# A hybrid decoder layer with 32 experts on one core: first weights by the block, second expert matrices in 16 KB packets, λ later, last sums earlier

## The chip, the cores and the metric

One core of a Trainium2 chip. The metric is the device time of one execution in microseconds; the time before is the median of three runs. All inputs and weights are fp32 in HBM.

## The reference, cut to what matters

```python
mod = silu(c) @ ada_w + ada_b                       # c: 1024, ada_w: 1024 x 6144
sh1, sc1, gt1, sh2, sc2, gt2 = split(mod, 6)
h = rms_norm(x, pre_mix_norm) * (1 + sc1) + sh1     # x: 256 x 1024
proj = h @ w_in                                     # attention and RWKV columns
...
lam = exp(sum(lam_q1 * lam_k1)) - exp(sum(lam_q2 * lam_k2)) + lambda_init
...
y = concatenate([y_da, y_rw]) @ w_out
x = x + gt1 * rms_norm(y, post_mix_norm)

h = rms_norm(x, pre_ffn_norm) * (1 + sc2) + sh2
logits = h @ router_w + router_b
top_vals, top_idx = top_k(logits, 4)                # of 32 experts
gates = sum(one_hot(top_idx, 32) * softmax(top_vals)[..., None], axis=1)
def expert(acc, w1_e, b1_e, w2_e, b2_e, g_e):       # w1: 1024 x 2048, w2: 1024 x 1024
    hid = h @ w1_e + b1_e
    glu, lin = min(hid[:, ::2], 7), clip(hid[:, 1::2], -7, 7)
    return acc + g_e[:, None] * ((glu * sigmoid(1.702 * glu) * (lin + 1)) @ w2_e + b2_e)
x = x + gt2 * rms_norm(sum over the experts, post_ffn_norm)
```

## The kernel before

**Mixer.** The program first computes the modulation rows sh1 and sc1, a pair of feature blocks of 128 at a time. `load_first(kp)` (L164) loads for pair `kp` two pieces of `ada_w` (shift and scale, 1 MB each, in runs of 1 KB) and two rows of blocks of `w_in` (896 KB each). `mod_rows` multiplies `cs` (silu of c) with a piece, `mod_copy` brings the row to SBUF, `mod_cols_first` turns it into columns `g1` and `sh1`, and `mod_x(k)` modulates block `k` of the transposed x into two halves, a high and a low one (`hpart`). `split_first` (L398) splits a block of `w_in` in the same way on ScalarE, VectorE and GpSimd. `proj_first(k, fs)` is the product of block `k`: 54 matmuls into seven PSUM banks, which were opened by a matmul with zeros. `warm(n)` issues `n` matmuls of ones whose result is not used. The order of PE, DVE and ACT in this part is that of the code. Attention and the RWKV heads follow; λ is worked out by five VectorE operations and one Exp (L729 to L736) when the last projection columns are shifted (`shift`).

**Experts.** The 32 experts run one after the other, the tokens of each gathered into 64, 32 or 96 slots (`kind`). An expert's weights are 12 MB: w1 as four pairs of blocks of 2 MB, w2 as four pieces of 1 MB. They go through a ring of 18 slots of 1 MB (`ring`, `slot`), and SyncE issues all loads in order (`load_expert`, L1577; pairs at L1598, w2 pieces at L1602). Each waits until PE has read what its slots held. The first four experts load w1 in single blocks.

Per expert: `gemm1` (eight blocks `k`, bias ahead of it), `act_of` (the clamped SwiGLU), `act_tr` (transposes), `gemm2` (eight blocks), `scatter` (products with `back` that spread the rows over the tokens, added into `acc` by VectorE at L1789). `gemm1` and `gemm2` call functions of a table `between` after certain blocks. In the last expert (p = 31) `sum_so_far(i)` opens the two final banks of token tile `i` with `acc` and the b2 term; the last `scatter` closes them, and `last_norm` writes the output. What its `gemm2` has between its blocks (`not nxt`):

```python
        elif not nxt:
            warm(24)
            between = {0: lambda: scatter(*done[:2], which=(0,)), 1: lambda: scatter(*done[:2], which=(1,)),
                       5: lambda: sum_so_far(0), 3: lambda: sum_so_far(1)}
```

All matmuls have the line of the helper `mm` (L104), transposes that of `tr` (L107). Tiles are named by use: `pair` are weight buffers, `xs` the gathered tokens, `aTt` the transposed activations, `ys` an expert's result.

Of the kernel before, what the change touches and what calls it, by code (L numbers as in the profile page):

```python
# [20 lines left out]
D = 1024  # L21
# [27 lines left out]
OVER_AT = 8  # L49
WARM = (34, 4, 0, 6, 8)  # L50
LEAD = 5
# [24 lines left out]
def hybrid_layer_kernel(ctx, tc, x, c, positions, ada_w, ada_b, pre_mix_norm, post_mix_norm,  # L76
# [26 lines left out]
    def mm(o, l, r, start=True, stop=True):  # L103
        PE.matmul(o, l, r, start=start, stop=stop)  # L104
# [60 lines left out]
    def load_first(kp):  # L165
# [23 lines left out]

    first = load_first(0)  # L190
    jp = pro.tile([128, 128], I32)
# [185 lines left out]
    def mod_cols_first(kp):  # L377
# [31 lines left out]

    ada, w = first  # L410
    warm(WARM[0])
    xj = pair((1024,), (1024,))
    norm_x(xj)
    x_tr(0, xj[0])
    mod_rows(0, 0, ada)
    x_tr(1, xj[1])
    mod_rows(0, 1, ada)
    col_tr(0)
    V.tensor_scalar(pc[:, cols["sc1"][0]:cols["sc1"][0] + 8], pc[:, cols["sc1"][0]:cols["sc1"][0] + 8], 1.0, None,
                    op0=OP.add)  # L420
    mod_copy(0)
    parts = []
    sf = split_first(w[:1], (G, V), (0, 512, 1024, 1536, 1792))
    for _ in range(2):
        next(sf)
    mod_cols_first(0)
    rwb = {}
    ORDER = (0, 2, 4, 6, 8, 10, 12)
    for f in ORDER:
        rwb[f] = (bankb if f in (12, 8, 10) else bank)()  # L430
        mm(rwb[f], zero, zero[:, 0:1].to_broadcast([128, 512]), True, False)
    warm(WARM[1], bankc)
    next(sf)
    mod_x(0)
    for _ in sf:
        pass
    mod_x(1)
    for _ in split_first(w[1:], (V, V)):
        pass
    first_order.close()  # L440


    mu1 = pro.tile([128, 14], F32)

    def shift(dst, p, f):
        S.activation(dst, p, AF.Copy, scale=mu1[:, f:f + 1])  # L446
        V.scalar_tensor_tensor(dst[:, 1:], p[:, 0:T - 1], col("mu", f), dst[:, 1:], op0=OP.mult, op1=OP.add)  # L447

    def proj_first(k, fs):
        xh, xl = hpart(k)  # L450
        for f in fs:
            for q in (f, f + 1):
                wh, wl = (t[:, q * 128:(q + 1) * 128] for t in parts[k])
                for n, (l, r) in enumerate(((wh, xh), (wh, xl), (wl, xh))):
                    mm(rwb[f][:, (q - f) * T:(q - f + 1) * T], l, r, False, k == KC - 1 and n == 2 and q > f)

    proj_order = tc.manual_schedule(engines={mybir.EngineType.PE, mybir.EngineType.DVE, mybir.EngineType.Activation})
    with proj_order:
        for kp in range(3):
            ada, w = load_first(kp + 1)  # L460
            k = 2 * kp
            proj_first(k, ORDER)
# [265 lines left out]
    lam2 = pro.tile([128, 2], F32)  # L728
    V.tensor_tensor(lamt[:, 0], lamt[:, 0], lamt[:, 1], op=OP.mult)  # L729
    V.tensor_tensor(lamt[:, 2], lamt[:, 2], lamt[:, 3], op=OP.mult)  # L730
    V.tensor_reduce(lam2, lamt[:, 0:4:2], axis=AX.X, op=OP.add)
    with tc.issue_after(first_act.ins):
        S.activation(lam2, lam2, AF.Exp)
    nlam = pro.tile([128, 1], F32)
    V.tensor_tensor(nlam, lam2[:, 1:2], lam2[:, 0:1], op=OP.subtract)
    V.tensor_scalar(nlam, nlam, LAMBDA_INIT, None, op0=OP.subtract)  # L736
    sub_c = pro.tile([128, 1], F32)
# [838 lines left out]

    def load_expert(e, s1_, s2_, single=False):  # L1577

# [5 lines left out]
        for j in range(4):  # L1584
# [148 lines left out]

    W2_ORDER = (0, 2, 1, 3)

    def gemm2(aTt, w2s, gates_of, kind, between=None):

        ks = [2 * s + j for s in W2_ORDER for j in range(2)]
        b64 = bank() if kind != 32 else None
# [35 lines left out]

    def scatter(ys, back, which=range(NT)):
        for i in which:
            for n in range(2):
                h = slice(64 * n, 64 * n + 64)
                if i in ends:  # L1780
                    for m, (j, y) in enumerate(ys):
                        mm(ends[i][n], back[h, j, i], y[h], False, m == len(ys) - 1)
                    continue
# [139 lines left out]
    for p in range(EXPERTS):  # L1923
        kind = kind_at(p)
        w1s, w2s = weights
        if p + 1 < EXPERTS:
            weights = [], {}
            rest_of_load = load_expert(expert_of(p + 1), *weights, p + 1 < SINGLE)
# [12 lines left out]
        if p + 1 < EXPERTS:  # L1941
# [14 lines left out]
            if 96 not in (kind, kind1):  # L1956
                bs = gemm1_bias(onehot(p + 1), kind1)
            between[5] = lambda: back1.append(prep_back(nxt[1], gate1, kind1, picked(p + 1)))
        back1 = []
        if p == 0:  # L1960
# [5 lines left out]

            between[3], between[5] = between[5], rest_of_first
# [18 lines left out]
        if p == OVER_AT:  # L1986
            last = nc.values_load(n_ov, min_val=0, max_val=MAX_OVER)
    scatter(*done[:2])
    pe_order.close()
# [66 lines left out]
```

## Time and profile before

| | us |
|---|---|
| median of 3 runs (lowest, highest) | 1189.94 (1188.75, 1190.77) |
| profiled execution, its own time | 1190.35 |
| its span in the trace | 1188.5 |
| PE busy | 1078.3 (91%) |
| VectorE busy | 412.1 (35%) |
| ScalarE busy | 227.6 (19%) |
| chain that ended last: DMA, PE | 45%, 45% |
| mean granted TensorE clock | 0.972 |

The span runs from the first to the last instruction; the run's own time has 1.85 us more around it. Busy shares are means over stages. The chain is followed back from the last instruction to what released each step. In rows, an arrow `<-` reads "out from in", and `x16` is a count of instructions.

### The profile page before, as it was taken

How to read it: one execution, taken by the hardware profiler on the slowest of the kernel's cores; microseconds unless marked ns; L12 is line 12 of the kernel's file. 1: busy time of each engine (PE TensorE's matmuls, PEld its weight loads, DVE VectorE, ACT ScalarE, POOL GpSimd, SP SyncE). 2: the span in 40 equal slices, each digit the busy share in tenths (PEclk: the TensorE clock that was granted, in tenths of full speed). 3: DMA queues.
4: the chain of work that ended last, by engine and by line, in shares of the span. 5: the costliest groups of instructions: out<-in, count | busy, mean ns of one | idle time of the engine just before them, and what ended most of it. 6: DMA issues, size and time to landing. Idle time of an engine off the chain costs nothing.

```text
span 1188.5 us, 17092 instructions
## 1 busy us (share of the span) xinstructions
PE 1078.3 (91%) x6717; PEld 507.3 (43%) x6717; DVE 412.1 (35%) x1114; ACT 227.6 (19%) x529; POOL 53.7 (5%) x100
## 2 busy tenths in 40 slices
PE   8999999999997877999988999988999999798765
PEld 6976667654343232233443233433333434333211
DVE  5688469852331212122323112312212223121203
ACT  4374353312011001010111010111010101101001
POOL 1331020000000000000000000000000000000000
PEclk8999999999999988999999999999999999999978
DMA  9862778899999999999999999999999999999991
GB/s 336 317 235 71 280 270 330 326 371 383 423 424 426 426 425 426 425 426 424 425 425 426 424 426 427 422 426 426 423 426 426 425 426 425 425 426 425 423 382 48
DMA packets 60101, 453.15 MB, mean 381 GB/s; under 512 B 7850, under 2 KB 16105, under 8 KB 23154
## 3 DMA queue, kind: packets, MB, share of 16 engines
q1 hardware_dynamic: 57970, 449.88, 91.9%
q0 software_dynamic: 1856, 2.13, 0.6%
q8 instruction: 54, 0.88, 0.3%
q14 instruction: 29, 0.24, 0.1%
q10 hardware_dynamic: 192, 0.02, 0.0%
HBM read 450.94 MB, written 1.06 MB: 380 GB/s over the span
## 4 chain that ended last, share of the span: by engine, by line
DMA 45%; PE 45%; DVE 6%; ACT 2%; issue 1%; SPq 0%; DVEq 0%; ACTq 0%
DMA pair<-in_moe_w 44%; PE bank L104 32%; PE bankb L104 10%; PE bankc L104 3%; DMA pair<-in_ada_w 1%; DVE pair L316 1%; PE bank L107 1%; ACT aTt L1731 0%; PE bankb L107 0%; DVE pair L447 0%; ACT xs L1656 0%; DVE w L316 0%; DVE pair L1195 0%; ACT pair L446 0%; DVE w L766 0%
## 5 line engine op out<-in xcount | busy, mean ns | idle before, releaser
L104 PE MATMUL bank<-pair,xs 128*64 128x512 f32 (+1 forms) x2240 | 408.6, 616 | 64.2 <-DMA pair<-in_moe_w 64.1
L104 PEld LDWEIGHTS bank<-pair,xs 128*64 128x64 f32 (+1 forms) x2240 | 114.5, 127 | 346.0 <-issue 241.3
L104 PE MATMUL bank<-pair,aTt 128*64 128x512 f32 (+1 forms) x1120 | 227.9, 618 | 12.0 <-ACT aTt L1731 10.7
L1676 DVE TENSOR_SCALAR glu<-bank 128x256 f32<-128x256 f32 x55 | 23.1, 420 | 397.2 <-PE bank L104 397.1
L1679 ACT ACTIVATE act<-glu 128x256 f32<-128x256 f32 x55 | 22.9, 417 | 464.8 <-DVE glu L1676 464.8
L1789 DVE TENSOR_TENSOR acc<-acc,bankb 128x512 f32<-128x512 f32 x120 | 77.4, 681 | 94.6 <-PE bankb L104 94.6
L104 PEld LDWEIGHTS bank<-pair,aTt 128*64 128x64 f32 (+1 forms) x1120 | 53.2, 126 | 124.9 <-issue 101.2
L104 PEld LDWEIGHTS bankb<-sel,own 128*128 128x128 f32 x608 | 73.5, 198 | 14.7 <-DVE glu L1676 9.0
L104 PE MATMUL bankb<-sel,own 128*128 128x96 f32 (+3 forms) x608 | 76.4, 285 | 0.0
L1759 ACT ACTIVATE ys<-bank,gs 128x512 fp32r<-128x512 f32 x32 | 22.0, 687 | 261.2 <-PE bank L104 261.2
L1760 DVE SCALAR_TENSOR_TENSOR ys<-bank,gs,ys 128x512 fp32r<-128x512 f32 x32 | 24.0, 751 | 106.2 <-ACT ys L1759 106.2
L104 PE MATMUL bankb<-ys,back 64*128 64x512 f32 x254 | 55.8, 449 | 4.7 <-DVE acc L1789 3.5
L1656 ACT ACTIVATE xs<-bankb,s2c,g2c 128x128 f32<-128x128 f32 (+2 forms) x136 | 48.3, 436 | 42.4 <-PE bankb L104 42.4
L1651 DVE TENSOR_SCALAR back<-bankb,pcol 128x256 fp32r<-128x256 f32 x35 | 16.6, 483 | 87.6 <-PE bankb L104 87.6
L104 PEld LDWEIGHTS bankb<-ys,back 64*128 64x128 f32 x254 | 25.8, 191 | 42.3 <-issue 26.0
L104 PE MATMUL bankb<-w,w 128*128 128x512 f32 (+3 forms) x120 | 30.9, 366 | 0.0
L1731 ACT ACTIVATE aTt<-bank 128x256 f32<-128x256 f32 x55 | 19.2, 386 | 50.6 <-PE bank L107 50.4
L104 PE MATMUL bankb<-w,own 128*128 128x512 f32 x80 | 27.3, 424 | 0.0
L104 PE MATMUL bank<-own,pair 128*128 128x256 f32 x128 | 26.6, 293 | 0.0
L104 PE MATMUL bank<-pair,pair 32*32 32x32 f32 (+4 forms) x400 | 26.1, 246 | 0.1
L104 PE MATMUL bankc<-pair,cs 128*32 128x256 f32 (+1 forms) x256 | 24.6, 493 | 1.4 <-DMA pair<-in_ada_w 1.4
L107 PE MATMUL bank<-ident,act 128*128 128x128 f32 x110 | 22.4, 315 | 2.4 <-DVE act L1681 2.4
(482 smaller groups left out, 1011.0 us busy)
## 6 DMA issues: line engine op xcount, KB each, us to landing
pair<-in_moe_w SPq DMA_DIRECT2D x112, 2048.0 KB
pair<-in_moe_w SPq DMA_DIRECT2D x160, 1024.0 KB
pair<-in_ada_w SPq DMA_DIRECT2D x24, 1024.0 KB
pair<-in_w_in SPq DMA_DIRECT2D x8, 896.0 KB
pair<-in_w_in SPq DMA_DIRECT2D x6, 1024.0 KB
pair<-in_w_out SPq DMA_DIRECT2D x4, 1024.0 KB
own<-in_x SPq DMA_DIRECT2D x2, 512.0 KB
own<-in_x SPq DMA_DIRECT2D x1, 1024.0 KB
```

The lines of the kernel that those rows point to most:

```text
L104: PE.matmul(o, l, r, start=start, stop=stop)
L107: PE.transpose(o, i, ident[0:i.shape[0], 0:i.shape[0]])
L316: last_lo = lo_eng.tensor_tensor(lo, src, hi.bitcast(F32), op=OP.subtract)
L1651: V.tensor_scalar(back[:, j], b3, pcol32[:, j:j + 1] if j or kind == 32 else pcol64, None, op0=OP.is_equal)
L1656: S.activation(xs[:, k, :cap], b, AF.Identity, scale=g2c[:, k:k + 1], bias=s2c[:, k:k + 1])
L1676: V.tensor_scalar(glu, v[:, :, 0], 7.0, None, op0=OP.min)
L1679: S.activation(dst, glu, AF.Tanh, scale=0.851)
L1731: S.activation(aTt[:, j0:j0 + 2], b[:, :256].rearrange("p (a b) -> p a b", a=2), AF.Copy)
L1759: S.activation(yh, b, AF.Copy, scale=gs[:, j:j + 1])
L1760: V.scalar_tensor_tensor(yl, b, gs[:, j:j + 1], yh.bitcast(F32), op0=OP.mult, op1=OP.subtract)
L1789: V.tensor_tensor(a, a, b, op=OP.add)
```

## The change

1. **First weights.** The first two feature blocks are loaded block by block: 512 KB of shift and 512 KB of scale (runs of 512 B) and `w_in` for block 0, then the same for block 1. `proj_first(0)` moves ahead, interleaved with block 1's modulation; the opening with zeros is split into four and three; four warming matmuls go.
2. **b1.** The expert biases `b1q` (256 KB) are loaded on ScalarE's queue at the start, not later on SyncE's, and permuted by four matmuls with 0/1 matrices (`ztile`).
3. **w2.** Experts 4 to 30 load w2 as two pieces of 2 MB in runs of 16 KB, where there were four of 1 MB in runs of 8 KB. The last expert has three of 1 MB and two of half a MB. `gemm2` goes through the blocks in order. So that the activations come out in the order that w2 now has, `gemm1` reads its moving operand w1 with a stride: runs of four fp32, every second one.
4. **λ** is worked out behind the last `shift`.
5. **Last expert.** Both `sum_so_far` and the scatter of expert 30, which goes into the final banks, move from `gemm2` into `gemm1` (behind blocks 1, 3 and 5), and 24 warming matmuls become 10.

```diff
-WARM = (34, 4, 0, 6, 8)
+WARM = (34, 10, 0, 6, 8)
...
+    def load_very_first():
+        ada, w = ([raw(2, KC, 128) for _ in range(2)], [raw(RWC) for _ in range(2)])
+        for k in range(2):
+            for j in range(2):
+                nc.sync.dma_start(ada[k][:, j], ada_r[:, :, j * D + k * 128:j * D + (k + 1) * 128])
+            nc.sync.dma_start(w[k], w_in[0, k * 128:(k + 1) * 128, RW0:RW0 + RWC])
+        return ada, w
...
-        nc.sync.dma_start(b1q, moe_b1[0].rearrange("e (q n) -> (e q) n", q=4))
+    S.dma_start(b1q, moe_b1[0].rearrange("e (q n) -> (e q) n", q=4))
...
-    x_tr(0, xj[0])
-    mod_rows(0, 0, ada)
-    x_tr(1, xj[1])
-    mod_rows(0, 1, ada)
-    col_tr(0)
...
-    warm(WARM[1], bankc)
...
+    bp = bankb()
+    for q in range(2):
+        for n in range(2):
+            mm(bp[:, q * 256:(q + 1) * 256], ztile[:, q, n],
+               b1q.rearrange("q (m n f) -> q n m f", n=2, f=4)[:, n], not n, n == 1)
+    x_tr(0, xj[0])
+    col_tr(0)
+    first_rows(0, ada[0])
+    S.activation(b1q, bp, AF.Copy)
+    x_tr(1, xj[1])
...
+    clear(*ORDER[:4])
...
+    first_copy(0)
...
+    first_cols(0)
+    clear(*ORDER[4:])
+    next(sf)
+    mod_x(0)
...
+    proj_first(0, ORDER[:3])
+    first_rows(1, ada[1])
+    first_copy(1)
+    proj_first(0, ORDER[3:5])
+    first_cols(1)
+    mod_x(1)
+    proj_first(0, ORDER[5:])
...
+    later.enter_context(tc.issue_after(last_shift.ins))
+    V.tensor_tensor(lamt[:, 0], lamt[:, 0], lamt[:, 1], op=OP.mult)
...
-        for n, k in enumerate(W2_ORDER):
-            yield
-            s = s2_[k] = slot((at + KC + n) % N_SLOTS, (2, D))
-            nc.sync.dma_start(s, w2[k * 256:(k + 1) * 256, :].rearrange("(p k) n -> p k n", k=2))
+        for j in range(2):
+
+            d = ring[(at + KC + 2 * j) % N_SLOTS // 2]
+            s = w2[j * 512:(j + 1) * 512, :].rearrange("(p k) n -> p k n", k=4)
+            for h in range(2):
+                s2_[2 * j + h] = view(d[:, h], (2, D))
+                yield
+                if single or last:
+
+                    for n in range(2) if last and j and h else (slice(0, 2),):
+                        nc.sync.dma_start(s2_[2 * j + h][:, n], s[:, 2 * h:2 * h + 2][:, n])
+                elif h:
+                    nc.sync.dma_start(d.rearrange("p k n -> p (k n)"), s.rearrange("p k n -> p (k n)"))
...
-            for o, s, c0 in parts(bs, kind):
-                mm(o, xs[:, k, s], w1s[k][:, c0:c0 + 512], False, k == KC - 1)
+            w = w1s[k].rearrange("p (h m n f) -> p h n m f", h=2, n=2, f=4)
+            for o, s, h, n in parts(bs, kind):
+                mm(o, xs[:, k, s], w[:, h, n], False, k == KC - 1)
...
+        if p == EXPERTS - 1:
+            between = {1: lambda: sum_so_far(0), 3: lambda: sum_so_far(1), 5: lambda: scatter(*done[:2])}
...
-            warm(24)
-            between = {0: lambda: scatter(*done[:2], which=(0,)), 1: lambda: scatter(*done[:2], which=(1,)),
-                       5: lambda: sum_so_far(0), 3: lambda: sum_so_far(1)}
+            warm(WARM[1])
+            between = {}
```

On SyncE's queue, the first loads of the program. Before, where `pair_87` and `pair_89` are the two 1 MB pieces of `ada_w` for blocks 0 and 1:

```order
L161 DMA own<-in_x 128x1024 x2
L169 DMA pair_87<-in_ada_w 128x8x256
L169 DMA pair_89<-in_ada_w 128x8x256
L173 DMA pair_91<-in_w_in 128x1792
L173 DMA pair_93<-in_w_in 128x1792
L169 DMA pair_307<-in_ada_w 128x8x256
```

Now, where `pair_87` is block 0's and `pair_88` block 1's:

```order
L161 DMA own<-in_x 128x1024 x2
L182 DMA pair_87<-in_ada_w 128x8x128 x2
L183 DMA pair_89<-in_w_in 128x1792
L182 DMA pair_88<-in_ada_w 128x8x128 x2
L183 DMA pair_90<-in_w_in 128x1792
L169 DMA pair_379<-in_ada_w 128x8x256
```

Ahead of block 0's `w_in` there is now 1 MB of `ada_w`, not 2 MB.

On PE, behind the 34 warming matmuls. Before (`ident,pair` are the transposes of x, `pair_87,cs` and `pair_89,cs` the shift and scale rows of both blocks, `q,w` their columns):

```order
L107 MATMUL bank<-ident,pair_174 128x128 x8
L104 MATMUL bankc<-pair_87,cs 32x256 x8
L107 MATMUL bank<-ident,pair_174 128x128 x8
L104 MATMUL bankc<-pair_89,cs 32x256 x8
L107 MATMUL bankb<-ident,prow_85 128x24
L104 MATMUL bankc<-q_115,w_221 128x1 x4
```

Now:

```order
L104 MATMUL bankb<-b1q,w_131 128x256 x4
L107 MATMUL bank<-ident,pair_183 128x128 x8
L107 MATMUL bankb<-ident,prow_85 128x24
L104 MATMUL bankc<-pair_87,cs 32x128 x16
L107 MATMUL bank<-ident,pair_183 128x128 x8
```

The permutation of b1 stands ahead of the first transposes, and block 0's shift and scale come in one go between the two groups of transposes.

On PE, in the last expert. Before, in `gemm2` behind the transposes (`pair,aTt` are its products, `ys,back` the scatter of expert 30, `acc,ident` and `pair,pgT` the sums):

```order
L104 MATMUL bank<-pair_1159,aTt 32x512 x2
L104 MATMUL bankb<-ys,back 128x512 x4
L104 MATMUL bank<-pair_1159,aTt 32x512 x2
L104 MATMUL bankb<-ys,back 128x512 x4
L104 MATMUL bank<-pair_1159,aTt 32x512 x4
L104 MATMUL bankb<-acc,ident 128x512
L104 MATMUL bankb<-pair_776,pgT 128x512
L104 MATMUL bankb<-acc,ident 128x512
L104 MATMUL bankb<-pair_776,pgT 128x512
L104 MATMUL bank<-pair_578,aTt 32x512 x4
```

Now, in `gemm1` (`pair,xs` are its products):

```order
L104 MATMUL bank<-pair_2726,xs 32x512 x8
L104 MATMUL bankb<-acc,ident 128x512
L104 MATMUL bankb<-pair_805,pgT 128x512
L104 MATMUL bankb<-acc,ident 128x512
L104 MATMUL bankb<-pair_805,pgT 128x512
L104 MATMUL bank<-pair_2727,xs 32x512 x8
L104 MATMUL bankb<-acc,ident 128x512
L104 MATMUL bankb<-pair_805,pgT 128x512
L104 MATMUL bankc<-acc,ident 128x512
L104 MATMUL bankc<-pair_805,pgT 128x512
L104 MATMUL bank<-pair_2728,xs 32x512 x8
L104 MATMUL bankb<-ys,back 128x512 x6
```

The sums and the scatter of expert 30 now stand between the w1 pairs, and `gemm2`'s products follow each other.

## Rows read from the trace of the kernel before

**Rows 1.** Stretches: us, each engine's busy time, PE clock, DMA share, GB/s

```profile
15.70:22.50 6.80, 6.80 (x26) 4.68 (x27) 4.51 (x10) 4.50 (x8) 2.85 (x2) 0.52 1.08 361
66.00:276.00 210.00, 200.22 (x1676) 138.88 (x1677) 150.33 (x449) 89.55 (x216) 21.33 (x42) 0.98 0.73 272
320.00:1137.00 817.00, 742.52 (x4108) 289.75 (x4100) 195.79 (x447) 98.96 (x241) 11.49 (x31) 0.98 1.01 425
1137.00:1142.00 5.00, 3.64 (x16) 0.60 (x16) 0.00 (x0) 0.00 (x0) 0.00 (x0) 0.50 1.02 433
```

**Rows 2.** Waits of SyncE's queue, the longest group: total us, times, longest us

```profile
SPq L1598 <- DMA pair<-in_moe_w: 371.4, 96, 5.7
```

**Rows 3.** The chain in the experts: start us, us, what

```profile
347.00 29.41 DMA pair<-in_moe_w
...
435.64 29.39 DMA pair<-in_moe_w
```

**Rows 4.** PE in time, last expert's gemm1: start, us, what, [idle before <-releaser]

```profile
1137.24 3.64 PE L104 MATMUL bank<-pair,xs 128*32 128x512 f32 x16 [4.28 <-DMA pair<-in_moe_w]
1142.15 3.45 PE L104 MATMUL bank<-pair,xs 128*32 128x512 f32 x16 [1.27 <-DMA pair<-in_moe_w]
1147.04 1.92 PE L104 MATMUL bank<-pair,xs 128*32 128x512 f32 x16 [1.44 <-DMA pair<-in_moe_w]
1151.93 3.53 PE L104 MATMUL bank<-pair,xs 128*32 128x512 f32 x16 [2.96 <-DMA pair<-in_moe_w]
1155.39 2.84 PE L104 MATMUL bank<-ones 128*128 128x256 bf16 x24
```

**Rows 5.** The chain in the last expert's gemm2: start us, us, what

```profile
1159.00 1.05 PE bank L104 x4
1160.05 0.67 PE bankb L104 x4
...
1163.37 4.21 PE bankb L104 x8
...
1172.79 1.04 PE bank L104 x8
```

**Rows 6.** VectorE in time, end of the last SwiGLU

```profile
1156.83 0.42 DVE L1681 SCALAR_TENSOR_TENSOR act<-act,lin 128x256 f32<-128x256 f32 x1
```

**Rows 7.** PE in time, the first modulation rows

```profile
10.42 1.07 PE L104 MATMUL bankc<-pair,cs 128*32 128x256 f32 x16 [0.62 <-DMA pair<-in_ada_w]
11.42 1.09 PE L107 MATMUL bank<-ident,pair 128*128 128x128 f32 x8
13.29 1.07 PE L104 MATMUL bankc<-pair,cs 128*32 128x256 f32 x16 [0.78 <-DMA pair<-in_ada_w]
```

**Rows 8.** The chain in the prologue: columns, openings, projection

```profile
15.69 1.84 PE bankc L104 x8
17.53 1.73 PE bank L104 x4
19.26 1.28 PE bankb L104 x3
...
21.39 3.31 PE bank L104 x24
...
28.26 1.86 PE bankc L104 x32
```

**Rows 9.** VectorE in time: split of block 1's w_in, and a step of λ

```profile
21.91 2.09 DVE L407 TENSOR_TENSOR pair<-pair,pair 128x896 fp32r<-128x896 f32 x2
...
71.92 0.27 DVE L731 TENSOR_REDUCE lam<-lamt 128x2 f32<-128x128 f32 x1
```

**Rows 10.** Weight loads of transposes, by form: count, busy us, mean ns, idle before

```profile
L107 PEld LDWEIGHTS bank<-ident,act 128*128 128x128 f32 x110 | 16.4, 207 | 13.7 <-issue 4.6 <-PE bankb L104 3.7 <-DVE act L1681 3.7
...
L107 PEld LDWEIGHTS bankb<-ident,w 128*128 128x128 f32 x36 | 3.9, 140 | 5.6 <-issue 2.6 <-DVE w L801 1.1 <-ACT w L726 0.9
```

**Rows 11.** gemm1's matmuls between 320 and 1137 us: count, busy us, mean ns, idle

```profile
L104 PE MATMUL bank<-pair,xs 128*32 128x512 f32 (+1 forms) x1976 | 359.6, 608 | 54.2 <-DMA pair<-in_moe_w 54.2
```

More of the change, by code (lines that the diff above doesn't have):

```diff
@@ L188, in load_cols @@
             ncol[g] += n
-    first = load_first(0)
+    first = load_very_first()
     jp = pro.tile([128, 128], I32)
@@ L298, in hybrid_layer_kernel @@
     load_cols(0, S, ((("sh1", "sc1"), ada_b[0, 0:2 * D]), (("pre_mix",), pre_mix_norm[0])))
+    S.dma_start(b1q, moe_b1[0].rearrange("e (q n) -> (e q) n", q=4))
     ident = const.tile([128, 128], F32)
     V.tensor_scalar(ident, jp, 0.0, None, op0=OP.is_equal)
+    ztile = w4s(2, 2, 128)
+    V.memset(ztile, 0.0)
+    for n in range(4):
+        V.tensor_copy(ztile[:, n // 2, n % 2, n % 2:128:2], ident[:, n // 2:128:2])
     last_act = None
@@ L389, in mod_cols_first, with first_rows, first_copy, first_cols @@
         V.tensor_tensor(sh1[:, ks], b[:, 0:2], pc[:, o:o + 2], op=OP.add)
+    def first_rows(k, ada):
+        if k == 0:
+            mod_of[0] = [None, w4s(4, 256)]
+        b = mod_of[0][0] = bankc()
+        for j in range(2):
+            for n in range(KC):
+                r = slice(32 * (n % 4), 32 * (n % 4) + 32)
+                mm(b[r, j * 128:(j + 1) * 128], cs[:, n:n + 1].to_broadcast([128, 32]), ada[:, j, n], n < 4, n >= 4)
+    def first_copy(k):
+        b, m = mod_of[0]
+        V.tensor_copy(m[:, 0:2, k * 128:(k + 1) * 128], b[:, 0:256].rearrange("p (a b) -> p a b", a=2))
+    def first_cols(k):
+        m = mod_of[0][1]
+        b = bankc()
+        for j in range(2):
+            mm(b[:, j:j + 1], m[:, j, k * 128:(k + 1) * 128], q32)
+        V.scalar_tensor_tensor(g1[:, k:k + 1], b[:, 1:2], col("sc1", k), col("pre_mix", k), op0=OP.add, op1=OP.mult)
+        V.tensor_tensor(sh1[:, k:k + 1], b[:, 0:1], col("sh1", k), op=OP.add)
     def mod_x(k):
@@ L408, in split_first @@
                 yield
[L410 to L413, printed above, removed]
-    x_tr(0, xj[0])
-    mod_rows(0, 0, ada)
-    x_tr(1, xj[1])
-    mod_rows(0, 1, ada)
-    col_tr(0)
[L419 to L431, printed above, removed]
-    warm(WARM[1], bankc)
[L433 to L447, printed above, removed]
     def proj_first(k, fs):
@@ L455, in proj_first, with clear, shift @@
                     mm(rwb[f][:, (q - f) * T:(q - f + 1) * T], l, r, False, k == KC - 1 and n == 2 and q > f)
+    ada, w = first
+    warm(WARM[0])
+    xj = pair((1024,), (1024,))
+    norm_x(xj)
+    bp = bankb()
[8 more added lines that the diff above has]
+    x_tr(1, xj[1])
+    rwb = {}
+    ORDER = (0, 2, 4, 6, 8, 10, 12)
+    def clear(*fs):
+        for f in fs:
+            rwb[f] = (bankb if f in (12, 8, 10) else bank)()
+            mm(rwb[f], zero, zero[:, 0:1].to_broadcast([128, 512]), True, False)
+    clear(*ORDER[:4])
+    V.tensor_scalar(pc[:, cols["sc1"][0]:cols["sc1"][0] + 8], pc[:, cols["sc1"][0]:cols["sc1"][0] + 8], 1.0, None,
+                    op0=OP.add)
+    first_copy(0)
+    parts = []
+    sf = split_first(w[:1], (G, V), (0, 512, 1024, 1536, 1792))
+    for _ in range(2):
+        next(sf)
+    first_cols(0)
+    clear(*ORDER[4:])
+    next(sf)
+    mod_x(0)
+    for _ in sf:
+        pass
+    proj_first(0, ORDER[:3])
[5 more added lines that the diff above has]
+    proj_first(0, ORDER[5:])
+    for _ in split_first(w[1:], (V, V)):
+        pass
+    first_order.close()
+    mu1 = pro.tile([128, 14], F32)
+    last_shift = None
+    def shift(dst, p, f):
+        nonlocal last_shift
+        last_shift = S.activation(dst, p, AF.Copy, scale=mu1[:, f:f + 1])
+        V.scalar_tensor_tensor(dst[:, 1:], p[:, 0:T - 1], col("mu", f), dst[:, 1:], op0=OP.mult, op1=OP.add)
     proj_order = tc.manual_schedule(engines={mybir.EngineType.PE, mybir.EngineType.DVE, mybir.EngineType.Activation})
@@ L461, in hybrid_layer_kernel @@
             k = 2 * kp
-            proj_first(k, ORDER)
+            if kp:
+                proj_first(k, ORDER)
             proj_first(k + 1, ORDER[:2])
@@ L1153, in hybrid_layer_kernel @@
     rkr, gB = rT, gT
+    later = ExitStack()
+    later.enter_context(tc.issue_after(last_shift.ins))
+    V.tensor_tensor(lamt[:, 0], lamt[:, 0], lamt[:, 1], op=OP.mult)
+    V.tensor_tensor(lamt[:, 2], lamt[:, 2], lamt[:, 3], op=OP.mult)
+    V.tensor_reduce(lam2, lamt[:, 0:4:2], axis=AX.X, op=OP.add)
+    S.activation(lam2, lam2, AF.Exp)
+    V.tensor_tensor(nlam, lam2[:, 1:2], lam2[:, 0:1], op=OP.subtract)
+    V.tensor_scalar(nlam, nlam, LAMBDA_INIT, None, op0=OP.subtract)
+    later.close()
     fill()
@@ L1574, in slot, with load_expert @@
         return view(ring[n // 2][:, n % 2], shape)
-    def load_expert(e, s1_, s2_, single=False):
+    def load_expert(e, s1_, s2_, single=False, last=False):
         w1 = moe_w1[0][e] if isinstance(e, int) else moe_w1[0][bass.ds(e, 1)].rearrange("o k n -> (o k) n")
@@ L1732, in act_tr @@
         return aTt
-    W2_ORDER = (0, 2, 1, 3)
     def gemm2(aTt, w2s, gates_of, kind, between=None):
-        ks = [2 * s + j for s in W2_ORDER for j in range(2)]
+        ks = range(KC)
         b64 = bank() if kind != 32 else None
@@ L1774, in hybrid_layer_kernel, with scatter @@
     summed = set()
-    def scatter(ys, back, which=range(NT)):
+    def scatter(ys, back, which=range(NT), last=False):
         for i in which:
@@ L1781, in scatter @@
                     for m, (j, y) in enumerate(ys):
-                        mm(ends[i][n], back[h, j, i], y[h], False, m == len(ys) - 1)
+                        mm(ends[i][n], back[h, j, i], y[h], False, last and m == len(ys) - 1)
                     continue
@@ L1927, in hybrid_layer_kernel @@
             weights = [], {}
-            rest_of_load = load_expert(expert_of(p + 1), *weights, p + 1 < SINGLE)
+            rest_of_load = load_expert(expert_of(p + 1), *weights, p + 1 < SINGLE, p + 2 == EXPERTS)
             next(rest_of_load)
@@ L1957, in hybrid_layer_kernel @@
                 bs = gemm1_bias(onehot(p + 1), kind1)
-            between[5] = lambda: back1.append(prep_back(nxt[1], gate1, kind1, picked(p + 1)))
+            between[3] = lambda: back1.append(prep_back(nxt[1], gate1, kind1, picked(p + 1)))
         back1 = []
@@ L1965, in rest_of_first @@
                 back = prep_back(sel_, gate0, 64, picked(0))
[L1967 removed]
+            between[1], between[3] = between[3], rest_of_first
         elif not nxt:
[L1969 to L1971 removed]
+            warm(WARM[1])
+            between = {}
         elif not early:
@@ L1987, in hybrid_layer_kernel @@
             last = nc.values_load(n_ov, min_val=0, max_val=MAX_OVER)
-    scatter(*done[:2])
+    scatter(*done[:2], last=True)
     pe_order.close()
```

12 lines of the change are left out of this document (3 added, 9 removed).

## The prediction, made before the run

> **What bounds the kernel now.** I read the stretches first. From 320 to 1137 us the DMA engines are busy throughout and move 425 GB/s, while PE is busy for 742.5 of 817 us [rows 1]. SyncE's longest wait, at the line that issues the w1 pairs, is for earlier transfers of expert weights: 371.4 us in 96 waits [rows 2]. The chain says the same, as one DMA step per expert: from 347.00 to 435.64 us it passes three periods, so an expert takes 88.64/3 = 29.55 us [rows 3]. Here bytes and their rate set the time, and PE has 74.5 us in hand. Ahead of it, from 66 to 276 us, it is the other way round: PE is busy for 200.2 of 210 us and the DMA share is 0.73 [rows 1], since slots come free at PE's pace. So the end is the sum of three things: how soon PE is through the mixer, the time of the bytes that are then left, and what follows the last weights. Each part of the change acts on one of them, and they add.
>
> **The tail.** Before, the last four w1 pairs land where the last gemm1's groups start: 1137.24, 1142.15, 1147.04 and 1151.93 [rows 4]. PE waits 1.3 to 4.3 us ahead of each. gemm2 then starts at 1159.00 and ends at 1172.79 + 1.04 = 1173.83, 14.8 us in which the scatter of expert 30 and both sums lie between its products (a sum is 4.21, a quarter of the scatter's two halves 0.67) [rows 5]. By itself gemm2 is four groups of 1.05, so 4.2 us.
>
> After, sums and scatter fill the waits of gemm1. From the same first landing: 1137.24 + 3.64 (pair 0) = 1140.88; + 4.21 (sum) = 1145.09; + 1.92 (pair 1, landed at 1142.15) = 1147.01; + 4.21 = 1151.22; + 1.92 = 1153.14; + 2 x 0.67 = 1154.48; + 1.92 (pair 3, landed at 1151.93) = 1156.40. All at full clock but the first. The clock, though, stands at 0.50 from 1137 to 1142 us [rows 1], and the first sum begins inside that stretch; if 1 us of it still runs at half speed, that costs 1 us more: 1157.4. At full half speed it would be 4.21.
>
> From gemm1's end to gemm2's start it took 1159.00 - 1155.39 = 3.6 us; 24 warming matmuls were 2.84 of it [rows 4], but the SwiGLU ended at 1156.83 + 0.42 = 1157.25 [rows 6], 1.9 us behind gemm1. With 10 of them (1.2 us) the SwiGLU ends last, and 3.6 becomes 3.6 - (2.84 - 1.9) = 2.7, or stays at 3.6. gemm2 starts at 1160.1 to 1161.0 and ends at 1164.3 to 1165.2. The last w2 bytes don't hold it: four MB behind 1151.93 at 2.45 us each (half of a pair's 4.897 = (1151.93 - 1137.24)/3 [rows 4]) are there at 1161.7, and only the last quarter of gemm2 (1.0 us) needs them. I take 1164.8: **-9.0 us**. Bounds: all at full clock and 2.7 us gives 1163.3 or -10.5; half speed through the whole first sum gives -6.
>
> **w2 in 16 KB runs.** A w1 pair, 2 MB in 16 KB runs, takes 4.897 us [rows 4]. An expert takes 29.55 [rows 3], of which four pairs are 19.59, which leaves 9.96 for the 4 MB of w2 in 8 KB runs; at the pairs' rate they would be 9.79. The difference is 0.16 us an expert, for 27 experts **-4.4 us**. It is small against how well I know it: 0.16 is 0.5% of a period, so the bounds are 0 and -5.6 (0.21 an expert). A wait that it adds: a 2 MB load needs both slots of its pair, where a 1 MB load needed one. In the bound stretch SyncE waits for older transfers most of all, so a slot that comes a little later shortens its lead alone; I price that at nothing. If the lead were used up, one load would start up to 2.45 us late per expert.
>
> The Trainium skill, in "DMA: Bandwidth & Descriptors", section Specifications, has full line rate from 512 B per transfer on; by it 8 KB runs have nothing to gain, and this term would be 0. This trace has less than that at 8 KB, if 9.96 against 9.79 us is no accident.
>
> **Strided reads in gemm1.** To match w2's order, gemm1 reads w1 in runs of four fp32 (16 B), every second one. No matmul of before does this. Nearest rows, both weight loads of transposes: a load that reads every second fp32 takes 207 ns, one that reads without a gap 140 [rows 10]. By the upper bound, x 1.48 on gemm1's 359.6 us [rows 11], PE would need 173 us more between 320 and 1137 us, 98 us more than it has in hand. The lower bound is nothing. I take nothing: the row's stride splits every group of four fp32, the change's doesn't. What covers a small loss is PE's 74.5 us; from 74.5/359.6 = 21% on it would be on the path.
>
> The Trainium skill, in "SBUF — State Buffer", section "Door 1: The DMA port swizzle", says that SBUF is read in lines of 16 B, at full rate when two accesses fall into one line; it counts four fp32 as the stride that is free. By it a stride of two would have been free as well, and the 207 against 140 ns disagree for weight loads; for the change's whole lines rule and my choice give the same sum.
>
> **The prologue.** Before, PE starts block 0's and 1's shift rows at 10.42 us and the scale rows at 13.29, as each MB lands: 2.87 us for a MB in 1 KB runs [rows 7], against 2.45 in 16 KB runs. After, x and two pieces of 512 KB are ahead, as many bytes as before 10.42. Runs of 512 B may cost another 0.4 us (one such step as from 16 to 1 KB), and the 256 KB of b1 on ScalarE's queue 0.7 us (0.25 x 2.87): 11.5 us, 1.8 earlier than 13.29. From there to the end of proj_first(0), PE has: block 0's rows 0.6 (half of 1.07), transposes 1.09 [rows 7], the openings 1.73 + 1.28 = 3.0, both blocks' columns 1.84, block 1's rows 0.6, 54 matmuls 28.26 - 21.39 = 6.87 [rows 8], 0.2 for the small transpose: 14.2 us, to 25.7. Before they ended at 28.26 [rows 8]. That is 2.5 us of gain at most, and two things eat at it. The clock was at 0.52 from 15.70 to 22.50 us with PE fully busy [rows 1], and 54 matmuls that start some 3 us sooner run for as much longer in it, for about 1.5 us. Block 1's modulation is now inside the projection, with its steps on VectorE behind block 0's split; I allow 1 us for PE's waits. That makes 28.2: **0.0**. Bounds: -2.5 without either, and +2 if VectorE holds up block 1: its low half of w_in, 2.09 us [rows 9], is what the next matmuls wait for.
>
> Behind it PE is dense up to 276 us, so what is won or lost here reaches the end. The permutation of b1 runs while PE waits for ada_w.
>
> **λ.** Five short VectorE steps such as the 0.27 us sum [rows 9] leave a stretch where VectorE runs back to back, to one with gaps: **-0.2 us**, between 0 and -0.5.
>
> **Sum.** -9.0 - 4.4 + 0.0 - 0.2 = -13.6. The profiled execution took 1190.35 (its span is 1188.5, 1.85 less), so it gives 1176.75. The median of the runs is 0.41 below the profiled one; **1176.3** is forecast for it.
>
> **Rivals.**
> - Longer runs give nothing, the line rate being reached: 1176.3 + 4.4 = 1180.7. For it: 425 GB/s all along, so little is left to win. Against: the periods' 0.16 us.
> - The prologue gains its 2.5 us: 1173.8. For it: the bytes ahead of block 0 are halved. Against: the clock row.
> - The prologue loses 2 us: 1178.3. For it: VectorE's 2.09 us split; against: PE has other work.
> - The tail gives half, -4.5, since the clock stays at half speed through both sums (2 x 4.21 more, less the waits they still fill): 1180.8. For it: 0.50 at the start of the last gemm1; against: PE has no gap once the sums fill the waits, and in the prologue the clock rose under such work.
> - The other side: strided reads slow gemm1 by over 21%, and PE becomes the bound. The place is each expert's gemm1; at the row's x 1.48 the packets' gain vanishes too, and the time is 1190.35 - 9.2 + 98 = about 1279. From 1.25 on (90 - 74.5 = 15 us) it eats all gains. For it: 207 against 140 ns; against: 16 B stay together.
>
> **How the numbers follow.** Forecast 0.55 (with 1172 to 1179 for the spread of its terms); no gain from runs 0.13; prologue gains 0.10; prologue loses 0.08; half a tail 0.07; slow strided reads 0.07. Leaving out the last and the outer ends of the first, the range is 1171.8 to 1182. Only strided reads put the time at or over before's; 0.2%, 2.4 us, is about what a measurement of this kernel can tell from no change: faster 0.92, same 0.02, slower 0.06.
>
> **What would show it.** The period of the chain per expert falls from 29.55 to 29.39 (runs). The last gemm1's groups stand with sums of 4.2 us between them and gemm2's four groups take 4.2 us without a gap (tail). proj_first(0) ends near 28.2 us (prologue). The gemm1 group stays near 608 ns for one (strided reads): over 730 would make the prediction wrong, as would a period set by PE, a second sum at half clock, or an end of proj_first(0) beyond 30 us.

## The result, and the profile after

| | before | changed |
|---|---|---|
| median of 15 runs (lowest, highest), us | 1190.1 (1186.85, 1192.12) | 1182.85 (1175.25, 1186.84) |
| profiled execution (its span), us | 1190.35 (1188.5) | 1184.62 (1182.5) |
| mean granted TensorE clock | 0.972 | 0.959 |

The ratio of the times is 0.9931, 95% interval 0.991 to 0.9951: faster by 7 us, where 13.6 were forecast. A second set of 12 runs of the same kernel gave 0.9935 (0.9905 to 0.9965). Against the shown 1189.94 the ratio makes 1181.7, 5.4 us above the forecast and 0.3 us inside the upper end of the range.

Two stretches of the changed kernel's profile, with the columns of [rows 1], and between them three more in which the clock was low:

```profile
10.00:15.00 5.00, 4.49 (x13) 3.70 (x14) 0.60 (x1) 0.00 (x0) 0.00 (x0) 0.50 1.10 354
66.00:276.00 210.00, 199.71 (x1661) 139.83 (x1660) 150.96 (x450) 87.55 (x211) 24.28 (x50) 0.97 0.72 265
135.00:147.00 12.00, 10.95 (x170) 9.04 (x168) 2.10 (x3) 4.63 (x10) 0.78 (x2) 0.72 0.70 265
190.00:200.00 10.00, 9.14 (x71) 6.86 (x70) 7.79 (x30) 2.92 (x6) 0.00 (x0) 0.83 1.02 417
320.00:1137.00 817.00, 761.03 (x4153) 298.88 (x4157) 198.88 (x456) 99.34 (x242) 11.49 (x31) 0.96 1.01 427
```

The rate in the experts (the last line) rose from 425 to 427 GB/s, as the packets' term wants. But from 66 to 276 us the DMA engines moved less, 265 GB/s where [rows 1] have 272: PE, which sets the pace there, was late. How late is read at one piece of work that both chains have, the first long gemm1 near 300 us. First the chain of the kernel before (start us, us, what):

```profile
300.13 11.25 PE bank L104 x82
```

Then the chain of the changed kernel, the prologue, this piece, and the last expert:

```profile
3.26 7.11 DMA b1q<-in_moe_b
...
10.51 3.75 PE bankb L104 x8
14.26 1.71 PE bank L107 x8
...
31.35 1.86 PE bankc L104 x32
...
307.23 11.25 PE bank L104 x82
...
1141.99 3.19 PE bank L104 x16
1145.18 4.59 PE bankb L104 x8
1149.78 1.85 PE bank L104 x16
1151.63 2.11 PE bankb L104 x4
1153.74 2.11 PE bankc L104 x4
1155.84 1.85 PE bank L104 x16
...
1158.84 1.90 PE bank L104 x16
...
1163.60 4.02 PE bank L104 x32
```

The reader is to see three things. The piece behind the prologue's 54 matmuls starts at 31.35, not at 28.26 [rows 8]: 3.1 us late, and the chain runs through the load of b1, which is new on it. (Those 54 are the 42 of block 0 and the first 12 of block 1; `proj_first(0)` by itself has 42.) At 300 us PE is 307.23 - 300.13 = 7.1 us late, so another 4 us were lost between. And from the last expert's first pair to the end of gemm2 it takes 1163.60 + 4.02 - 1141.99 = 25.6 us, where before had 1173.83 - 1137.24 = 36.6 [rows 4, 5]: 11.0 us won. (The second profile of the changed kernel has 26.3, so 10.3.) Between 307 and 1142 us the lag went from 7.1 to 1141.99 - 1137.24 = 4.75 [rows 4].

### The profile page after: what moved, and what is told of

The parts are those of the page before. It is cut to its first block, busy times and chain, and to the rows that moved or that the text cites. A ratio compares the mean times of both kernels' runs of the same rounds, so it can differ in the third digit from the quotient of the medians.

```text
span 1182.5 us, 16914 instructions
## 1 busy us (share of the span) xinstructions
PE 1090.9 (92%) x6738; PEld 516.9 (44%) x6739; DVE 410.5 (35%) x1117; ACT 228.0 (19%) x530; POOL 53.6 (5%) x100
## 4 chain that ended last, share of the span: by engine, by line
PE 61%; DMA 28%; DVE 7%; ACT 3%; issue 1%; ACTq 0%; DVEq 0%; SPq 0%
PE bank L104 43%; DMA pair<-in_moe_w 27%; PE bankb L104 13%; PE bankc L104 2%; PE bank L107 1%; DVE pair L330 1%; DMA b1q<-in_moe_b 1%; ACT aTt L1800 1%; PE bankb L107 0%; DVE pair L510 0%; DVE acc L1856 0%; ACT xs L1723 0%; ACT pair L1156 0%; DVE pair L1253 0%; DVE act L1748 0%
## 5 line engine op out<-in xcount | busy, mean ns | idle before, releaser
L104 PE MATMUL bank<-pair,aTt 128*64 128x512 f32 (+1 forms) x1120 | 232.4, 641 | 13.2 <-ACT aTt L1800 10.7
L1856 DVE TENSOR_TENSOR acc<-acc,bankb 128x512 f32<-128x512 f32 x116 | 74.9, 682 | 97.0 <-PE bankb L104 96.9
L104 PEld LDWEIGHTS bankb<-sel,own 128*128 128x128 f32 x608 | 79.0, 210 | 14.7 <-DVE glu L1743 9.0
L104 PE MATMUL bankb<-sel,own 128*128 128x96 f32 (+3 forms) x608 | 81.9, 297 | 0.0
L104 PE MATMUL bankc<-pair,cs 128*32 128x512 f32 (+2 forms) x288 | 25.3, 467 | 0.0
```

What stands on the lines that cost most here:

```text
L1856: V.tensor_tensor(a, a, b, op=OP.add)
```

## The experiments

Theory A: the tail and the packets came as forecast; what is missing was lost ahead of 300 us, in the prologue to b1's permutation, on which PE waits in its order, and in the mixer to stretches of low clock. Rivals: the loads by the block cost the prologue (B); the tail was small and the packets large (C); 2 MB loads lose what their rate wins (D). All ratios are to the kernel before.

**Without b1.** The kernel leaves out the permutation, and b1 is loaded late, on SyncE's queue.

```diff
-    S.dma_start(b1q, moe_b1[0].rearrange("e (q n) -> (e q) n", q=4))
+        nc.sync.dma_start(b1q, moe_b1[0].rearrange("e (q n) -> (e q) n", q=4))
...
-    bp = bankb()
-    for q in range(2):
-        for n in range(2):
-            mm(bp[:, q * 256:(q + 1) * 256], ztile[:, q, n],
...
-    S.activation(b1q, bp, AF.Copy)
```

> The changed kernel without the early load and the permutation of b1 (b1 is loaded on SyncE's queue as before and not permuted; the permutation is left out of the computation). Theory A: b1 alone made the prologue late. The first transposes of x then start near 9 us, not 14.05, the last matmul of proj_first(0) ends 3 to 6 us before 31.35, and the run is 3 to 6 us shorter than the changed kernel. Theory B: the loads by the block, in 512 B runs, made it late. The end of proj_first(0) stays within 1 us of 31.35 and the time within 1 us of the changed kernel's.

The median is 1179.67, the ratio 0.9906 (0.9874 to 0.9938). PE in time, and the end of the prologue in the chain:

```profile
8.86 1.09 PE L107 MATMUL bank<-ident,pair 128*128 128x128 f32 x8 [2.41 <-DVE pair L356]
11.02 0.64 PE L104 MATMUL bankc<-pair,cs 128*32 128x128 f32 x16 [0.33 <-DMA pair<-in_ada_w]
```

```profile
25.84 1.86 PE bankc L104 x32
```

The transposes start at 8.86, not 14.26, and the piece behind the prologue at 25.84: 5.5 us earlier than in the changed kernel and 2.4 earlier than before. B falls; A's step holds in the trace. The ratio moved by 0.25%, 3 us, with intervals that overlap, so the times alone don't show it. This profile lost much of it again, in a stretch at half clock:

```profile
160.00:183.00 23.00, 22.38 (x179) 14.56 (x178) 11.52 (x32) 9.75 (x30) 3.96 (x6) 0.55 0.55 174
```

**Old prologue, without b1.** The loads and PE's order of before in the prologue, no permutation, the rest as changed.

```diff
-    first = load_very_first()
+    first = load_first(0)
...
```

> The changed kernel with the prologue of before (ada_w by the pair, 1 KB runs, order of before) and without the early load and the permutation of b1 (the permutation is left out of the computation). Theory A: without b1 the new order of the prologue is the better one, by the 2.4 us that its end lies ahead of before's in the run without b1 (25.84 against 28.26). So proj_first(0) ends near 28.3 here and the run is 2 to 3 us longer than the one without b1. Theory B: the loads by the block give nothing of their own, so the two agree within 1 us.

Median 1176.78, ratio 0.989 (0.9859 to 0.9921): not slower than the run without b1. In its chain:

```profile
15.49 1.02 PE bankc L104 x8
16.51 1.31 PE bank L104 x4
...
26.55 1.86 PE bankc L104 x32
```

Here the old prologue ends at 26.55 and not at 28.26, since the clock came up sooner: the columns took 1.02 us where [rows 8] have 1.84. Before's second profile has 29.43, with the second piece of `ada_w` 1.5 us later than in [rows 7]. So the new order by itself is worth 0.7 us against this run, 2.4 against [rows 8] and 3.6 against that profile: no loss, but A's 2 to 3 us don't show in the times, and the prologue of before varies too much for these runs to size the gain.

**Permutation later.** The four matmuls stand behind the first columns; the early load stays.

```diff
...
-    clear(*ORDER[4:])
+    clear(*ORDER[4:6])
+    for q in range(2):
+        for n in range(2):
+            mm(bp[:, q * 256:(q + 1) * 256], ztile[:, q, n],
+               b1q.rearrange("q (m n f) -> q n m f", n=2, f=4)[:, n], not n, n == 1)
...
```

> The changed kernel with the four permuting matmuls moved behind the first columns, into PE's wait ahead of proj_first(0); the early load stays. Theory A: what costs is that PE's first transposes stand behind b1 in its order, so this wins nearly as much as leaving b1 out, 2.5 to 5 us. Theory B: the load itself, 256 KB beside ada_w, and the 512 B runs cost, so at most 1 us is won.

Ratio 0.9933 (0.9904 to 0.9962): nothing won. The permutation took 1.89 us and the prologue ended at 26.75, ahead of before's, but then PE and VectorE in time show:

```profile
15.10 1.89 PE L104 MATMUL bankb<-b1q,w 128*128 128x256 f32 x8
...
70.13 1.91 PE L104 MATMUL bankc<-w,pair 65*128 65x512 f32 x2 [3.34 <-ACT pair L1123]
```

```profile
67.94 0.62 DVE L1207 TENSOR_TENSOR lamt<-lamt 128x64 f32<-128x64 f32 x1 [2.27 <-DMA lamt<-in_da_lambda_k]
```

The scheduler had put λ's steps ahead of the shifts, at 65 us, where VectorE stood 2.27 us at λ's own loads; PE waited 3.34 us behind it, where the changed kernel waits 0.52. Right behind this wait stood a stretch at half clock (granted clock 0.57 from 70 to 78 us), in which PE lost another 1.8 us against the changed kernel; a second one, from 241 to 251 us, is in this profile too. So λ's wait is not all of the miss. The run was made again with λ held back.

**Permutation later, λ held.** `one` is 0 times a late tile plus 1.

```diff
...
+    one = pro.tile([128, 1], F32)
+    V.tensor_scalar(one, fac[:, 0:1], 0.0, 1.0, op0=OP.mult, op1=OP.add)
+    V.scalar_tensor_tensor(lamt[:, 0], lamt[:, 0], one, lamt[:, 1], op0=OP.mult, op1=OP.mult)
...
```

> The changed kernel with b1's permutation in PE's wait ahead of proj_first(0), as in the run before, and with lambda held behind 80 us by a factor 1 that is made from a tile of that time, since in that run VectorE stood 2.27 us at lambda's loads. Theory A: nothing then eats what the later permutation wins: the lag behind before is -1.3 us at 43 us and still -2 to -3 at 100 us, against +2.4 in the changed kernel. Its median is 3 to 5 us below the changed kernel's, near 1179. Rival: the loss moves on to another wait, and the lag at 100 us is above -1.

Median 1177.37 (1174.71 to 1179.7), ratio 0.99 (0.9881 to 0.9918). In its chain:

```profile
26.77 1.86 PE bankc L104 x32
...
297.69 11.24 PE bank L104 x82
```

At 300 us it is 2.4 us ahead of before and 9.5 and 5.4 ahead of the changed kernel's two profiles. Of the lead over the first, 4.6 us are the prologue's (26.77 against 31.35); and this profile has no low clock at all from 31 to 300 us, which the next run of the same kernel need not repeat. It computes all of the reference. Its median, of 6 runs, is 5.4 us below the changed kernel's; its interval ends at 0.9918, where the changed kernel's two begin at 0.991 and 0.9905, so it is probably the better of the two.

**The tail of before.** Sums and scatter back in gemm2, 24 warming matmuls.

> The changed kernel with the last expert as before: sums and scatter in gemm2, 24 warming matmuls. Theory A: the tail's term was 9 us as predicted or somewhat more (the traces say 10.96 from the first w1 pair's landing to gemm2's end), so this is 9 to 11 us slower than the changed kernel, 1191 to 1194. Theory C: the tail gave half of that, and the packets gave more: 4 to 6 us slower.

Median 1194.6, ratio 1.0015 (0.998 to 1.0049): 0.8% above the changed kernel, 10 us, with intervals that don't meet. A holds, C falls. In its chain the sums stand between gemm2's pieces again:

```profile
1162.73 6.29 PE bank L104 x40
...
1179.37 4.21 PE bankb L104 x8
1183.58 1.04 PE bank L104 x8
```

From the last pair to gemm2's end it is 1184.62 - 1162.73 = 21.9 us, as before (1173.83 - 1151.93 [rows 4, 5]).

**w2 in 8 KB runs.** `load_expert`'s four pieces of before, and gemm1 without the stride. b1 stays permuted, which no longer fits gemm1's columns:

```diff
...
-            w = w1s[k].rearrange("p (h m n f) -> p h n m f", h=2, n=2, f=4)
...
-                mm(o, xs[:, k, s], w[:, h, n], False, k == KC - 1)
+                mm(o, xs[:, k, s], w1s[k][:, c0:c0 + 512], False, k == KC - 1)
...
```

> The changed kernel with w2 in four pieces of 1 MB in 8 KB runs for every expert, and gemm1 reading without a stride, as before (b1 stays permuted, so the biases don't match). Theory A: the packets gave what the bytes say, 1.7 MB or 4 us of lead between 320 and 1130 us: 3.5 to 5 us slower than the changed kernel, 425 GB/s in place of 427. Theory D: loads of 2 MB, which need two free slots, start later when the DMA engines first catch up near 280 to 300 us, and lose there what the rate gains: within 1.5 us of the changed kernel.

Median 1188.33, ratio 0.9966 (0.9934 to 0.9998): about 0.3% above the changed kernel, 4 us, with intervals that overlap, so again the trace decides. Its stretch in the experts, then gemm1's group between 320 and 1137 us, of this run and of the changed kernel:

```profile
320.00:1137.00 817.00, 745.56 (x4130) 290.67 (x4132) 199.34 (x456) 99.43 (x243) 11.71 (x32) 0.98 1.01 425
```

```profile
L104 PE MATMUL bank<-pair,xs 128*64 128x512 f32 (+1 forms) x1984 | 362.3, 612 | 55.0 <-DMA pair<-in_moe_w 54.8
```

```profile
L104 PE MATMUL bank<-pair,xs 128*64 128x512 f32 (+1 forms) x1984 | 361.8, 614 | 37.5 <-DMA pair<-in_moe_w 37.4
```

425 GB/s again, so the 2 GB/s come with the runs' length: 2/425 of 817 us is 3.8 us. PE in time shows the period too, where a gemm1 waits for the same pair of two experts in a row, first in this run, then in the changed kernel:

```profile
385.45 3.34 PE L104 MATMUL bank<-pair,xs 128*32 128x512 f32 x16 [2.98 <-DMA pair<-in_moe_w]
414.97 3.65 PE L104 MATMUL bank<-pair,xs 128*64 128x512 f32 x16 [1.23 <-DMA pair<-in_moe_w]
```

```profile
384.83 3.54 PE L104 MATMUL bank<-pair,xs 128*32 128x512 f32 x16 [2.98 <-DMA pair<-in_moe_w]
414.21 3.65 PE L104 MATMUL bank<-pair,xs 128*64 128x512 f32 x16 [1.25 <-DMA pair<-in_moe_w]
```

That is 29.52 us an expert here and 29.38 there, so 0.14 x 27 = 3.8 us. The times of the DMA packets in the traces agree: from the first 90 MB to the first 425 MB the lag behind before goes from 7.8 to 4.1 us in the changed kernel, and stays at 8.7 in this run. D falls. The strided matmuls take 614 ns where these take 612: the stride costs next to nothing.

**λ early.** λ's steps where they were before, the rest as changed.

> The changed kernel with lambda worked out where it was before. Theory A: the traces show the lag behind before falling from 3.1 to 2.1 us between 73 and 78 us, so lambda's place is worth 1 us and not 0.2: the steps behind 78 us come about 1 us later than in the changed kernel; the time is 1 us longer, less than these runs can tell. Rival: that fall is chance, and the steps stay within 0.3 us.

Ratio 0.9951 (0.9914 to 0.9988), which tells nothing against 0.9935. The traces do. PE in time up to the first product with the tile `Lhl`, in this run, and that product in the changed kernel's second run, both with the prologue 3.3 us late:

```profile
79.91 1.22 PE L104 MATMUL bank<-trid,w 128*128 128x256 f32 x8 [1.03 <-ACT fac L1164]
...
103.08 1.09 PE L104 MATMUL bank<-Lhl,w 128*128 128x256 f32 x4 [1.48 <-ACT Lhl L329]
```

```profile
102.10 1.09 PE L104 MATMUL bank<-Lhl,w 128*128 128x256 f32 x4 [1.43 <-ACT Lhl L329]
```

λ's new place is worth 1.0 us. Most of it is the wait of 1.03 us for `fac` in the first row, which is 0.20 in the changed kernel.

**Both kernels again.**

> The changed kernel once more, to see what differs between its own runs. Theory A: low-clock stretches of TensorE in the mixer (139.0 and 193.6 us in the first profile) come and go from run to run and make up most of the spread of 1175 to 1187: in this profile they stand at other places or are absent, and the lag behind before at 276 us differs from the first profile's 7.1 by their length's share. Rival: they belong to the program, and stand at the same places with the same lag within 0.5 us.

> The kernel before once more, one profile. Theory A: its low-clock stretch at 100.8 us too is of the run and not of the program: it stands elsewhere, is longer or is absent, and the steps at 276 us are some us early or late against the first profile. Rival: the same place, within 0.5 us.

The changed kernel's second set has the median 1182.78. The piece near 300 us starts at 303.12 in its profile, 4.1 us earlier than in the first profile of the same kernel; before's second profile has it at 300.51, 0.4 later than its first. Two stretches of the changed kernel's second profile, then three of before's first: the two where its clock was low in the mixer, and between them one where the changed kernel's first had it low:

```profile
135.00:147.00 12.00, 11.22 (x199) 8.87 (x195) 2.87 (x4) 5.47 (x12) 0.78 (x2) 1.00 0.81 300
190.00:200.00 10.00, 9.61 (x62) 6.67 (x63) 7.52 (x24) 5.54 (x9) 0.00 (x0) 0.83 0.94 365
```

```profile
100.00:105.00 5.00, 4.93 (x23) 4.12 (x23) 4.96 (x10) 0.89 (x2) 0.95 (x1) 0.66 0.43 138
135.00:147.00 12.00, 12.00 (x147) 8.53 (x147) 3.31 (x4) 4.87 (x11) 0.78 (x2) 1.00 0.85 309
258.00:268.00 10.00, 9.95 (x51) 6.06 (x50) 5.28 (x23) 2.67 (x8) 0.48 (x1) 0.83 0.91 367
```

The clock fell at 139 us in one run of the changed kernel (0.72 over 12 us) and not in the other; near 190 to 194 us in both, at the same work. So A holds for the first and its rival for the second. In before it is the same mixture: its second profile has the low stretch of 100.8 us at 101.6, behind a prologue that ended 1.2 us later, but not the one of 261 us (granted clock 1.00 from 258 to 268).

**Warm waits.** The better kernel with warming matmuls in four kinds of wait of the mixer.

```diff
-WARM = (34, 10, 0, 6, 8)
+WARM = (34, 10, 6, 10, 12)
...
+        if s == 0:
+            for _ in range(11):
+                mm(b[:, 0:256], ones.bitcast(BF16)[:, 0:128], ones.bitcast(BF16))
...
```

> The kernel of the run above with unused warming matmuls in four of PE's waits of the mixer: 11 ahead of the products of Lhl (1.4 us wait), 6 ahead of each transpose group of the normalised attention, and 6, 10, 12 for 0, 6, 8 in the routing. Theory A: drops of TensorE's clock in the mixer begin behind such waits, so fewer of them come; the profile has no low-clock stretch between 95 and 110 and between 185 and 250 us, and the median falls by 1 to 3 us more. Rival: drops come from the tiny 32x32 products and not from the waits: the clock falls elsewhere between 130 and 185 us, and the time is the same or, by the cost of the added matmuls, up to 2 us longer.

Median 1175.33 (1173.28 to 1187.61), ratio 0.9904 (0.9869 to 0.9939): not to be told from the run without them. The profile has no low clock from 31 to 260 us, but the one without them hadn't either, so this settles nothing on the drops.

**Fewer first matmuls.** `WARM[0]` is 17 for 34.

> The changed kernel with 17 first warming matmuls for 34, so that 17 matmuls fewer stand ahead of everything in PE's program. Theory E: the wait of about 1 us near 138 us that the profile puts down to issue, in every kernel with the changed prologue and in none with before's, depends on where PE's program is cut for loading, since 35 more instructions stand ahead of that place: with 17 fewer it shrinks below 0.5 us or stands at another instruction. Rival: it belongs to the instruction and stays at 0.7 to 1.1 us.

PE in time, first of the changed kernel, then of this run:

```profile
136.45 0.74 PE L104 MATMUL bank<-pair 32*32 32x32 f32 x63
138.24 0.21 PE L104 MATMUL bank<-pair 32*32 32x32 f32 x1 [1.05 <-issue]
```

```profile
135.90 2.00 PE L104 MATMUL bank<-pair,w 128*128 128x64 f32 x16
138.60 0.74 PE L104 MATMUL bankb<-w,own 128*128 128x512 f32 x2 [0.70 <-issue]
```

In the changed kernel PE stands 1.05 us ahead of the 64th of the tiny products and waits for nothing that the profile shows. With 17 matmuls fewer ahead, the tiny products run through, and a wait of 0.70 us stands behind the sixteen products that follow them: 17 matmuls further on. In the run without b1, with 8 fewer ahead, it stands 8 further on, and in Warm waits, with 11 more than its base, 11 sooner. So it hangs on how many instructions stand ahead, not on the instruction: in all ten profiles that have it, it stands behind 1106 to 1108 recorded matmuls of PE. In all ten it ends 2.4 to 2.6 us after the start of a packet of 16 KB on the DMA queue that the page lists as `q8 instruction` (135.62 us in the changed kernel, where PE arrives at the place 1.6 us later). In the three profiles with the old prologue PE arrives some 5 us after the same packet (the eighth of that queue's 16 KB packets) and doesn't wait. Both point to the loading of PE's program as what PE waits for; no run moved the load itself.

## Why the prediction was right in direction and too large

**Tail.** The mechanism was right, the term too small: 11.0 us in the first profile, half a us beyond its outer bound of -10.5, 10.3 in the second, and 0.8% when undone, where 9.0 were forecast. The first sum took 4.59 for 4.21, so 0.4 us were lost to the clock, not 1, and pair 0 took 3.19 for 3.64; the SwiGLU set gemm2's start as worked out (1163.60, 2.9 us behind gemm1). gemm2 ran in one piece of 4.02 us.

**Packets.** 3.8 us by the rate and by the period, 4.4 forecast; the period fell to 29.38, where 29.39 was the sign. The Trainium skill's "DMA: Bandwidth & Descriptors", section Specifications, has full line rate from 512 B on; here a stream all in 16 KB runs moved 427 GB/s and one with a third of its bytes in 8 KB runs 425, a small difference that a kernel bound by its bytes for 817 us gets in full. Of PE's lag of 7.1 us at 300 us, though, only 2.4 were won back when the last expert's first pair landed, 1.4 less than 3.8. Half of that was there before: by its packets the DMA was 7.8 us behind at that time, not 7.1. The other 0.7 us are not traced.

**Strided reads.** Nothing that shows (614 against 612 ns), as taken. The 207 against 140 ns of [rows 10] were the wrong neighbour: there the stride splits groups of four fp32. That this makes the difference, and not that those are weight loads, is argued.

**λ.** 1.0 us for 0.2, because λ's steps stood ahead of `fac`, for which PE waited: the gaps on VectorE that I put them into were not the question, the wait behind them was. That is outside the bound of -0.5.

**The prologue.** This is the step that failed: "The permutation of b1 runs while PE waits for ada_w." PE had to wait for b1 itself until 10.51 us, not for `ada_w`: x's transposes stood behind the permutation in PE's order, though x was there, and its 8 matmuls took 3.75 us at half clock (0.50 from 10 to 15 us). In the run with the permutation later they took 1.89. The term was 0.0 with bounds -2.5 and +2, and came out at +3.1 against the first profile of before (+1.9 against the second); the end at 31.35 is beyond the 30 us that the prediction had named as a sign of being wrong. Without b1 the new order nearly reached the lower bound, -2.4, with the clock up throughout. I priced the load's bytes, 0.7 us, and not what was queued behind its wait. The rival with the prologue losing 2 us had another cause, VectorE's split of block 1; for that PE waited 0.32 and 0.63 us ahead of block 1's matmuls, as much as the 1 us that was allowed. One price in the sum was also too low: block 1's rows are two pieces and took 1.01 us (from 23.95 in the chain), not 0.6.

**The mixer.** No term stood for it. Of the 4.0 us lost between 31 and 300 us in the first profile, λ gave 1.0 back, PE's wait for issue cost 1.1, and low clock 3.4, which leaves 0.5. From 135 to 147 us the clock of 0.72 means (1.00 - 0.72)/0.50 x 12 = 6.7 us at the lower of its two levels, and from 190 to 200 us 3.4. Half of such a stretch is lost where PE is dense: 5.1 us, against 1.7 for before's stretch at 101 us (0.66 over 5 us, 3.4 us). Each of the two profiles has one more of 3.4 us, at 261 us before and at 269 us in the changed kernel; these cancel.

With the terms as measured, tail -11.0, packets -3.8, λ -1.0, prologue +3.1 and issue +1.1 make -11.6. In the first profile low clock, the 0.5 that it leaves and the 1.4 beside the packets add 5.3, which gives -6.3; the spans differ by 6.0. Over all runs the medians differ by 7.2, so something costs the changed kernel some 4 us more than the kernel before. In the first profile most of that is low clock; for the runs in general this is open. The mean granted clock of the runs doesn't tell: its median is 0.970 over 27 runs of the changed kernel and 0.971 over the 28 of before that were run beside the second set, and it counts stretches in the experts where PE waits for bytes anyway. The wait for issue lies just ahead of the stretch at 139 us in three profiles of ten that have it, and in the seven others no stretch follows, so it is not shown to be the cause. That the clock's drops could be prevented by filling waits was tried once and not settled.

That the time lies inside the range is in part luck: the prologue came out above its bound and the mixer's loss had no term, and the tail and λ, both better than their bounds, took 2.8 us of it back.

## What to carry to other kernels

A load that is moved to an idle queue is free only if nothing waits for it early: look at what its first reader has queued behind it on an in-order engine. Work that only needs earlier results belongs in the waits of the last DMA-bound stretch and not behind it; there most of it cost nothing (gemm1 ended at 1160.74, and by the landings of [rows 4] it would have ended near 1158.6 with nothing in between, an estimate). A step that the scheduler places can slide ahead of its own loads when the work before it gets shorter, so read the traces again after each edit.

## What the runs showed of the hardware that was not expected

PE had a wait of 0.5 to 1.7 us between 133 and 139 us in all ten profiles with the new prologue and in none of the three with the old one; in nine of the ten the profile shows nothing that it waited for. It stood behind 1106 to 1108 recorded matmuls of PE in all ten, and ended 2.4 to 2.6 us after the start of a packet of 16 KB on the queue `q8 instruction`.

The clock falls at different places in runs of one kernel and of its variants: the run without b1 had it at half from 161 to 182 us, the changed kernel at 139 us in one profile and not in the other, the run with λ held nowhere from 31 to 300 us. The changed kernel's 27 runs spread over 1175 to 1188 us; how much of that is the clock is not shown (their mean granted clocks run from 0.959 to 0.980, and the correlation with the time is -0.45). One profile alone would have put the mixer's part 4 us off.
